# Seven more seven-product couples in the down products of a two-layer encoder trunk, all weights' sums prepared ahead, and the preparation's transfers on GpSimd's queue

## The chip, the cores and the metric

The kernel runs on one core of a Trainium2 chip. The metric is the device time of one execution in microseconds (us). Three runs of the kernel before took 2364.60, 2366.93 and 2368.82 us; the median is 2366.93 us. One further execution was profiled.

## The reference

The model is a trunk of two layers on one sequence of 256 tokens with 2048 channels, all in float32. Each layer has a token mixer (layer 0 a bidirectional mLSTM, layer 1 a bidirectional gated linear recurrence) and then a convolutional gated MLP, each behind an RMSNorm and added to the residual:

```python
def conv_glu(hn, w_up, conv_w, conv_b, w_down):
    u = hn @ w_up                       # 2048 -> 2 x 5504
    a, v = jnp.split(u, 2, axis=-1)
    ...                                 # c: centred depthwise convolution of width 3 over a
    return (jax.nn.gelu(c, approximate=False) * v) @ w_down      # 5504 -> 2048

for layer in range(DEPTH):
    ...
    h = h + mix
    h = h + conv_glu(rmsnorm(h, norm_ffn_g[layer]), ...)
return rmsnorm(h, final_g)
```

The change touches the last product, `@ w_down`, which is called the down product below; its input (256 tokens by 5504) is called g.

## The kernel before, in words

**Three matmuls for one product.** Every operand x is split into a high part xh (fp32r) and a low part xl = x - xh. A product of x and w is the sum of xh·wh, xh·wl and xl·wh, three matmuls of 128 x 512 on TensorE (L236). Activations are split when they are made. Weights are split as they arrive: a raw piece of 128 x 1024 floats is copied to wh by ScalarE (L147) and wl = raw - wh is taken by VectorE (L148). A helper keeps pieces ahead of TensorE, in four buffers for wh and wl each and, in the MLP, two more.

**Chunks and stages.** TensorE's work is a list of chunks. In an MLP the 43 blocks of 128 hidden channels come in two parts of 22 and 21. Each part first has one up chunk for each block, and then two down chunks, each for 1024 of the 2048 output columns; two such down chunks that follow each other are a pair of chunks, and there are four pairs of chunks in all (two layers, two parts).

**Couples and seven products.** A down chunk (`squares_by_seven`) takes two blocks of g at a time, a couple. The 256 tokens x 256 channels of a couple and its 256 x 1024 weights form 2 x 2 squares, A11 to A22 and B11 to B22. A plain couple takes eight products, 24 matmuls, into the four accumulators C11, C12, C21, C22. A couple that is listed in `SEVEN` takes seven products, 21 matmuls, by a Strassen-Winograd scheme: P1, P6, P7 and P5 go to four accumulators of their own, and three go straight to C11, C12 and C21. It needs sums of the activations' squares S1 to S4 (`token_sums`) and sums of the weights' squares T2, T3, T4 and B12 - B11. The accumulators are PSUM banks: P1, P6, P7, P5 in four banks of the pool `psm` (tiles named mm), C11 to C22 in four of `psa` (tiles named pc). The eight banks are all there are, so the next chunk's accumulators can begin only when the last ones have been read out.

**Reading out.** When a down chunk has met its last seven-product couple, `mid` (L584 to L592) adds the four P banks into the residual hm: ScalarE copies P1 to u (L584), VectorE adds P1, P6, P5 (twice), u and P7 in six instructions of 128 x 512 (L585 to L590), GpSimd adds u to two squares of hm (L591, L592). At the end of the chunk `done` adds C11, C21, C12 and C22 on VectorE (L598). In the kernel before, `mid` is called with one plain couple (nine or ten couples in, of eleven) still to come.

**Where the weights' sums come from.** Either on the fly: four VectorE subtractions (L207) right before the couple, listed in `FLY`; or prepared: earlier, while an up stage or the mixer runs, the couple's raw weights (two transfers of 512 KB into tiles praw) are loaded, four subtractions are made on VectorE (L632), and the result is stored to a scratch tensor tscr (two transfers of 512 KB, L635). When the couple comes, three transfers bring 768 KB of raw weights, 768 KB of sums (tile T, L198) and 256 KB more (L199).

**Order.** Instructions are written in program order with a planner's ticks for the side work (`Side`); a list scheduler that works on an estimated timeline then sets the order on each engine. Each engine runs its instructions in that order. All weights' loads and, before the change, all transfers of the preparation inside the MLP are issued by SyncE (SP), which also issues in order and waits in order. There, loads of the preparation are pinned among the loads of up weights (`late`, L395).

## Time and profile before

| what | value |
|---|---|
| three runs, us | 2364.60, 2366.93, 2368.82 |
| profiled execution, span from first to last instruction | 2364.5 us |
| granted TensorE clock, mean | 0.999 |
| up stages (layer 0 part 0 and 1, layer 1 part 0 and 1), from us | 388.7, 742.1, 1663.7, 2017.3 |
| pairs of down chunks, from us | 634.2, 975.1, 1909.3, 2250.3 |
| DMA, mean over the span | 268 GB/s, 632.97 MB |
| instructions | 38407 |

The profile gives one time for the profiled execution, its span; no time around it is listed. A row of a group view has the line, the engine, the operation, the tiles (written <- read) and their shapes, the count, then busy us and the mean ns of one, then the idle time before it and what ended it. A row of the view by windows gives, for each engine, busy us and the number of instructions that ran, then the granted clock, the busy share of the 16 DMA engines, and GB/s. A row of the timeline has start in us, duration in us, engine, line, operation, tiles, count.

### The profile page before, as it was taken

The numbers are of one execution on the slowest core, as the hardware profiler recorded it, in microseconds if no ns is written. First come the engines' busy times: TensorE is split into PE (matmuls) and PEld (weight loads), VectorE is DVE, ScalarE is ACT, GpSimd is POOL, SyncE is SP. The second block draws the span as 40 slices with busy tenths as digits, with TensorE's granted clock in tenths as the row PEclk, the third lists the DMA queues.
The fourth block names the chain that finished last, engine by engine and source line by source line (L and its number), as shares of the span: only waits on it lengthen the run. The fifth ranks groups of instructions, "written<-read, shape, count | busy, mean of one in ns | idle before, by whom it ended". The sixth has DMA issues, their size and how long they took to land. (4 is left out here: it accounts for less than half of the span.)

```text
span 2364.5 us, 38407 instructions
## 1 busy us (share of the span) xinstructions
PE 2354.1 (100%) x14545; PEld 2016.2 (85%) x14545; DVE 1993.5 (84%) x3087; ACT 1470.0 (62%) x2340; POOL 196.5 (8%) x244
## 2 busy tenths in 40 slices
PE   9999999999999999999999999999999999999998
PEld 8888888888888888888888888888888888888887
DVE  7777687888998898897888888778789889888888
ACT  7655456555665555676777777776555567455565
POOL 0100000000000000000232322220000000000000
PEclk9999999999999999999999999999999999999999
DMA  8776656888888878996556665646788888888896
GB/s 303 239 248 242 213 195 211 295 282 292 313 321 327 306 282 292 330 334 230 208 203 223 212 225 204 214 169 228 270 300 289 289 321 335 295 287 302 309 351 221
DMA packets 122266, 632.97 MB, mean 268 GB/s; under 512 B 13776, under 2 KB 14928, under 8 KB 77664
## 3 DMA queue, kind: packets, MB, share of 16 engines
q1 hardware_dynamic: 120384, 626.51, 75.0%
q0 software_dynamic: 1120, 3.21, 0.8%
q8 instruction: 114, 1.87, 0.3%
q10 hardware_dynamic: 576, 0.79, 0.1%
q14 instruction: 72, 0.59, 0.1%
HBM read 562.24 MB, written 68.22 MB: 267 GB/s over the span
## 5 line engine op out<-in xcount | busy, mean ns | idle before, releaser
L357 PE MATMUL mm<-xt,wh 128*128 128x512 f32 x3776 | 1312.0, 394 | 0.0
L148 DVE TENSOR_TENSOR wl<-raw,wh 128x1024 fp32r<-128x1024 f32 (+1 forms) x844 | 1037.3, 1234 | 222.6 <-ACT wh L147 214.5
L147 ACT CAST wh<-raw 128x1024 fp32r<-128x1024 f32 (+1 forms) x844 | 875.3, 1042 | 513.0 <-PE mm L357 305.8
L361 PE MATMUL mm<-xt,wl 128*128 128x256 f32 x3776 | 1043.5, 278 | 0.0
L357 PEld LDWEIGHTS mm<-xt,wh 128*128 128x128 f32 x3776 | 705.6, 188 | 160.6 <-issue 0.4
L361 PEld LDWEIGHTS mm<-xt,wl 128*128 128x128 f32 x3776 | 709.4, 188 | 4.5
L373 PE MATMUL mm<-wh,xt 128*128 128x512 f32 x1024 | 324.4, 392 | 0.6 <-ACT wh L147 0.5
L236 PE MATMUL pc<-wh,g 128*128 128x512 f32 (+1 forms) x716 | 243.2, 388 | 0.3 <-ACT wh L147 0.2
L373 PEld LDWEIGHTS mm<-wh,xt 128*128 128x128 f32 x1024 | 191.2, 188 | 40.0 <-ACT wh L147 1.1
L632 DVE TENSOR_TENSOR praw<-praw 128x512 f32<-128x512 f32 x252 | 174.1, 691 | 44.7 <-DMA praw<-in_w_d 29.0
L373 PE MATMUL mm<-wl,xt 128*128 128x512 f32 x512 | 199.7, 391 | 0.0
L236 PEld LDWEIGHTS pc<-wh,g 128*128 128x128 f32 x716 | 134.1, 188 | 29.0 <-ACT wh L147 1.5
L236 PE MATMUL mm<-wh,sx 128*128 128x512 f32 x432 | 153.4, 389 | 0.0
L148 DVE TENSOR_TENSOR wl<-T,wh 128x1024 fp32r<-128x1024 f32 (+1 forms) x144 | 135.9, 955 | 13.3 <-ACT wh L147 8.9
L147 ACT CAST wh<-T 128x1024 fp32r<-128x1024 f32 (+1 forms) x144 | 118.6, 835 | 44.7 <-DMA T<-tscr 18.2
L236 PE MATMUL pc<-wl,g 128*128 128x512 f32 (+1 forms) x358 | 138.8, 388 | 0.0
L591 POOL TENSOR_TENSOR hm<-hm,u 128x512 f32<-128x512 f32 x10 | 14.8, 1481 | 1223.8 <-DVE u L590 1223.8
L373 PEld LDWEIGHTS mm<-wl,xt 128*128 128x128 f32 x512 | 96.2, 188 | 18.6
L1071 DVE TENSOR_TENSOR QK<-QK,G 128x256 f32<-128x256 f32 x224 | 104.6, 515 | 6.2 <-ACT kq L1050 5.9
L1195 ACT COPY avc<-mm 128x256 f32<-128x256 f32 x172 | 64.0, 372 | 63.9 <-PE mm L361 63.6
L1050 ACT COPY kq<-QK 128x512 f32<-128x512 f32 x112 | 74.5, 669 | 37.3 <-DVE QK L1071 29.5
L236 PEld LDWEIGHTS mm<-wh,sx 128*128 128x128 f32 x432 | 81.0, 188 | 16.9 <-ACT wh L147 0.2
(246 smaller groups left out, 2263.1 us busy)
## 6 DMA issues: line engine op xcount, KB each, us to landing
raw<-in_w_up SPq DMA_DIRECT2D x172, 1024.0 KB, 6.1
tscr<-praw SPq DMA_DIRECT2D x126, 512.0 KB, 6.7
praw<-in_w_d SPq DMA_DIRECT2D x120, 512.0 KB, 6.8
raw<-in_w_bq SPq DMA_DIRECT2D x48, 1024.0 KB, 5.0
T<-tscr SPq DMA_DIRECT2D x63, 768.0 KB, 7.6
raw<-in_w_d SPq DMA_DIRECT2D x60, 768.0 KB, 6.0
raw<-in_w_ao SPq DMA_DIRECT2D x24, 1024.0 KB, 4.8
raw<-in_w_d SPq DMA_DIRECT2D x24, 1024.0 KB, 7.7
```

The source lines that it names most:

```text
L147: pin(act.copy(wh[:, :m], r))
L148: pin(dve.tensor_tensor(wl[:, :m], r, wh[:, :m].bitcast(F32), ALU.subtract))
L236: pin(pe.matmul(ps, a, b, start=bank not in begun, stop=stop and i == 2))
L357: hold(pe.matmul(ps[f], wh[:, c:c + P], x, start=k + kk == 0, stop=False))
L361: hold(pe.matmul(ps[f][:, 0:T], wl[:, c:c + P], x[:, 0:T], start=False, stop=k + kk == ch.nk - 1))
L373: pe.matmul(ps[t], x[:, a + t * P:a + (t + 1) * P], w[:, c], start=st and i == 0, stop=sp and i == 2)
L591: pool.tensor_tensor(part(1, 0), part(1, 0), u, ALU.add)
L632: dve.tensor_tensor(out, x, y, ALU.subtract)
L1050: act.copy(m, blocks(QK, h))
L1071: dve.tensor_tensor(two[:, j], two[:, j], by[:, j], ALU.mult)
L1195: act.copy(z, p[:, T:2 * T])
```

## The change

Five things change together.

- `SEVEN` now lists, for each of the four pairs of chunks, the couples of its first and of its second down chunk apart. Before, both chunks of a pair had the same list; there were 2 x (9 + 8 + 9 + 7) = 66 couples. Now there are 10 + 10, 9 + 8, 10 + 10 and 9 + 7, which is 73. In part 0 of either layer the last couple of the chunk, number 10 of 0 to 10, is now a seven-product couple. In part 1 the chunk ends with a single block, and the couple before it is now one.
- `FLY` is gone: no sums on the fly. Six couples of the down chunks were made so; all 73 are now prepared.
- In a last seven-product couple the order of products is P1, P6, P7, P5, then `mid`, then the three that go to C (in part 1 C12 stands behind P1). The first couple of a chunk takes its four accumulators in the order C22, C12, C11, C21. C22 can stop at the last plain couple.
- The preparation in the MLP issues its transfers on GpSimd's queue (`pool.dma_start`, 122 loads and 122 stores), and loads two items ahead, each after the store that frees its buffer.
- To make room, `ones` shrinks to 128 columns, R has one buffer, gs shares the tile jk; where only one chunk of a pair uses a couple's sums, they get a tile of their own ("spare").

```diff
-SEVEN = ((1, 2, 3, 4, 5, 6, 7, 8, 9), (1, 2, 3, 4, 5, 6, 7, 8)), ((1, 2, 3, 4, 5, 6, 7, 8, 9), (1, 2, 3, 4, 5, 6, 7))
-FLY = (2,), (5,), (2,), ()
+SEVEN = (range(1, 11), range(1, 11)), (range(1, 10), range(1, 9)), (range(1, 11), range(1, 11)), (range(1, 10), range(1, 8))
 FIRST = 6
-SPLIT = (0, 2, 5), (0, 2, 5)
+SPLIT = 2, 1
...
         units, last = (ch.nk + 1) // 2, max(ch.seven)
+        alone = max(set(range(units)) - set(ch.seven))
...
-                    product(ps, x, w, u == last and ps in psm_)
+                    product(ps, x, w, u == last if ps in psm_ else end)
                     side.tick(0.65)
...
             if u in ch.seven:
                 S1, S3, S2, S4 = ch.sums(u)
-                products((P1, A11, B11), (C12, S4, B22))
+                products((P1, A11, B11))
+                if not end:
+                    products((C12, S4, B22))
                 T2, T3 = piece()
                 products((P6, S2, T2), (P7, S3, T3))
                 B21, T1 = piece()
-                products((C11, A12, B21), (P5, S1, T1))
-                T4, _ = piece()
-                products((C21, A22, T4))
+                products((P5, S1, T1))
                 if u == last:
                     ch.mid(psm_)
                     ch.rest = ch.ends
+                if end:
+                    products((C12, S4, B22))
+                products((C11, A12, B21))
+                T4, _ = piece()
+                products((C21, A22, T4))
                 continue
             B21, B12 = piece()
-            for ps, (x, w), (y, v) in ((C11, (A11, B11), (A12, B21)), (C12, (A11, B12), (A12, B22)),
-                                       (C21, (A21, B11), (A22, B21)), (C22, (A21, B12), (A22, B22))):
+            both = [(C11, (A11, B11), (A12, B21)), (C12, (A11, B12), (A12, B22)),
+                    (C21, (A21, B11), (A22, B21)), (C22, (A21, B12), (A22, B22))]
+            for ps, (x, w), (y, v) in [both[i] for i in ((3, 1, 0, 2) if u == 0 else range(4))]:
                 product(ps, x, w, False)
-                product(ps, y, v, end)
+                product(ps, y, v, end or ps is C22 and u == alone)
...
+        put = start if ahead else nc.sync.dma_start
         yield first
         load(0)
+        if ahead:
+            load(1)
         for i, (_, dst) in enumerate(todo):
             yield period / 2
-            if ahead:
-                load(i + 1)
...
             for j in range(2):
-                nc.sync.dma_start(dst[:, j * 1024:(j + 1) * 1024], loaded[i][j])
+                put(dst[:, j * 1024:(j + 1) * 1024], loaded[i][j])
+            if ahead:
+                load(i + 2)
             yield period / 3
...
-                                  todo, 18.0, (nf * 10.4 - 26.0) / len(todo), finished, late, True))
+                                  todo, 18.0, (nf * 10.4 - 26.0) / len(todo), finished, pool.dma_start, True))
```

**Place 1: VectorE at the end of the first down chunk of layer 0, part 0.** Tiles mm_6313 to mm_6316 are P1, P6, P7, P5 of the ending chunk and pc_6317 to pc_6320 its C11, C12, C21, C22; hm is the residual; wl_6726 and wl_6743 are the next chunk's first two weight pieces. Before:

```order
L585 TENSOR_TENSOR hm_75<-hm_75,mm_6313 128x512
L586 TENSOR_TENSOR u_6732<-u_6732,mm_6314 128x512
L587 TENSOR_TENSOR hm_75<-hm_75,mm_6316 128x512
L589 TENSOR_TENSOR hm_75<-hm_75,mm_6316 128x512
L588 TENSOR_TENSOR hm_75<-hm_75,u_6732 128x512
L148 TENSOR_TENSOR wl_6726<-raw_6723,wh_6725 128x1024
L590 TENSOR_TENSOR u_6732<-u_6732,mm_6315 128x512
L598 TENSOR_TENSOR hm_75<-hm_75,pc_6317 128x512
```

Now, where mm_6362 to mm_6365 are P1, P6, P7, P5, pc_6366 to pc_6369 are C11, C12, C21, C22, and wl_6790 and wl_6800 are the next chunk's first two pieces, wl_6828 and wl_6847 those behind them:

```order
L591 TENSOR_TENSOR hm_75<-hm_75,mm_6362 128x512
L593 TENSOR_TENSOR hm_75<-hm_75,mm_6365 128x512
L595 TENSOR_TENSOR hm_75<-hm_75,mm_6365 128x512
L147 TENSOR_TENSOR wl_6790<-raw_6787,wh_6789 128x1024
L604 TENSOR_TENSOR hm_75<-hm_75,pc_6366 128x512
L592 TENSOR_TENSOR u_6806<-u_6806,mm_6363 128x512
L147 TENSOR_TENSOR wl_6800<-raw_6787,wh_6799 128x1024
L594 TENSOR_TENSOR hm_75<-hm_75,u_6806 128x512
L147 TENSOR_TENSOR wl_6828<-raw_6822,wh_6827 128x1024
L147 TENSOR_TENSOR wl_6847<-T_6824,wh_6846 128x1024
L596 TENSOR_TENSOR u_6806<-u_6806,mm_6364 128x512
L604 TENSOR_TENSOR hm_75<-hm_75,pc_6367 128x512
```

The adds of P5 (mm_6365) come second and third, and everything behind them waits for P5's last matmul; the next chunk's second piece, wl_6800, stands behind four adds, and the adds of P6 and C are mixed with the new pieces.

**Place 2: TensorE at the same end.** Before, P5 (mm_6316) stops here, 26 matmuls of the last, plain couple follow, and then the next chunk begins with pc_6787; the last of these rows are

```order
L236 MATMUL pc_6320<-wl_6714,g20_6191 128x512
L236 MATMUL pc_6320<-wh_6713,g20_6191 128x512
L236 MATMUL pc_6320<-wh_6703,g21_6310 128x512
L236 MATMUL pc_6320<-wl_6704,g21_6310 128x512
L236 MATMUL pc_6320<-wh_6703,g21_6310 128x512
L236 MATMUL pc_6787<-wh_6725,g0_4006 128x512
```

Now the first row is P5's last matmul, nine matmuls follow, and the next chunk begins with pc_6845, whose bank is that of pc_6366:

```order
L235 MATMUL mm_6365<-wh_6773,sx_6353 128x512
L235 MATMUL pc_6366<-wl_6774,g21_6350 128x512
L235 MATMUL pc_6366<-wh_6773,g21_6350 128x512
L235 MATMUL pc_6368<-wh_6780,g21_6350 128x512
L235 MATMUL mm_6363<-wl_6764,sx_6353 128x512
L235 MATMUL mm_6363<-wh_6763,sx_6353 128x512
L235 MATMUL mm_6364<-wl_6764,sx_6353 128x512
L235 MATMUL mm_6364<-wh_6763,sx_6353 128x512
L235 MATMUL pc_6368<-wl_6781,g21_6350 128x512
L235 MATMUL pc_6368<-wh_6780,g21_6350 128x512
L235 MATMUL pc_6845<-wh_6799,g0_4006 128x512
L235 MATMUL mm_6838<-wh_6827,g2_4224 128x512
```

Between P5's last matmul and the next chunk's first there are 9 matmuls where there were 26.

**Place 3: VectorE at the end of the first down chunk of layer 0, part 1**, which closes with a single block of twelve matmuls. mm_9646 to mm_9649 are P1, P6, P7, P5; pc_9650 is C11; wl_10047 and wl_10067 are the next chunk's first two pieces. Now:

```order
L592 TENSOR_TENSOR u_10053<-u_10053,mm_9647 128x512
L593 TENSOR_TENSOR hm_75<-hm_75,mm_9649 128x512
L595 TENSOR_TENSOR hm_75<-hm_75,mm_9649 128x512
L594 TENSOR_TENSOR hm_75<-hm_75,u_10053 128x512
L147 TENSOR_TENSOR wl_10047<-raw_10044,wh_10046 128x1024
L147 TENSOR_TENSOR wl_10067<-raw_10044,wh_10066 128x1024
L596 TENSOR_TENSOR u_10053<-u_10053,mm_9648 128x512
L604 TENSOR_TENSOR hm_75<-hm_75,pc_9650 128x512
```

On TensorE 17 matmuls stand between P5's last matmul there and the first one that writes to the bank of pc_9650. Before, there was a plain couple between the last seven-product couple and the single block, and 38 matmuls stood between P5's last one and the next chunk's first one that reads its first block of g.

34 lines of the change are left out of this document (20 added, 14 removed).

## The prediction

> **What bounds the kernel now.** I read the page first, then TensorE's waits, then the windows of the stages, then the timeline at the places that the change rewrites.
>
> ```profile
> span 2364.5 us, 38407 instructions
> PE 2354.1 (100%) x14545; PEld 2016.2 (85%) x14545; DVE 1993.5 (84%) x3087; ACT 1470.0 (62%) x2340; POOL 196.5 (8%) x244
> PE idle L1266 <- POOL ones L1259: 1.1, 1, 1.1
> PE mm L236 <- DVE wl L148: 0.5, 1, 0.5
> PE mm L373 <- ACT wh L147: 0.5, 2, 0.3
> PE pc L236 <- ACT wh L147: 0.2, 1, 0.2
> ```
>
> TensorE is busy all the time. Its waits add up to 2.3 us in 2364.5, and only 0.7 of them are in the down product (L236). So the time is TensorE's list of matmuls: one matmul less is a gain of its whole step, and a wait that the change makes is paid in full, for there is no slack on TensorE in which it could vanish. What else is full shows in the windows (the pairs of down chunks of layer 0 part 0 and of layer 1 part 0, the first up stage, and 20 us in each of the two pairs):
>
> ```profile
> 634.20:742.10 107.90, 107.83 (x476) 88.95 (x475) 99.29 (x112) 73.18 (x86) 3.54 (x2) 1.00 0.86 321
> 1909.30:2017.30 108.00, 107.78 (x476) 88.80 (x475) 102.50 (x117) 72.93 (x87) 3.55 (x2) 1.00 0.88 325
> 388.70:634.20 245.50, 245.50 (x1421) 214.76 (x1420) 213.81 (x349) 141.12 (x223) 0.70 (x1) 1.00 0.85 294
> 650.00:670.00 20.00, 20.00 (x90) 16.57 (x89) 16.64 (x17) 14.56 (x18) 0.00 (x0) 1.00 1.01 405
> ```
>
> In a pair of down chunks VectorE is busy 99.29 of 107.90 us and 102.50 of 108.00, the DMA engines 0.86 and 0.88. Neither stops TensorE on average, but neither has much left for a crowded moment. The step of a 128x512 matmul is 107.9 / 476 = 0.2267 us (a record is longer, 0.39, since matmuls overlap). The clock is 1.00 throughout, so it makes no difference here.
>
> **The change part by part.** *Matmuls removed.* Seven couples go from 24 to 21 matmuls: 21 x 0.2267 = **-4.8 us**, all of it on TensorE. That is the whole prize.
>
> *On-the-fly sums removed.* TensorE loses time at two of the six couples that were made on the fly:
>
> ```profile
> 699.59 0.61 PE L236 MATMUL mm<-wh,sx 128*128 128x512 f32 x2
> 700.28 0.50 PE L236 MATMUL pc<-wh,g 128*128 128x512 f32 x1
> 700.62 0.40 PE L236 MATMUL mm<-wh,sx 128*128 128x512 f32 x1
> 1930.43 0.69 PE L236 MATMUL mm<-wh,sx 128*128 128x512 f32 x2
> 1931.33 0.50 PE L236 MATMUL pc<-wh,g 128*128 128x512 f32 x1 [0.22 <-ACT wh L147]
> 1931.67 0.40 PE L236 MATMUL mm<-wh,sx 128*128 128x512 f32 x1
> ```
>
> Three steps take 1.03 and 1.24 us there instead of 0.68: 0.35 + 0.56 lost, **-0.9 us**. A stall also costs about 0.11 after it (the step behind it is 0.34, not 0.227). The other four couples lose nothing now, so nothing comes back there.
>
> *Preparation of 13 more couples, in the up stages.* Four units or three more per stage, each with four subtractions on VectorE:
>
> ```profile
> L632 DVE TENSOR_TENSOR praw<-praw 128x512 f32<-128x512 f32 x252 | 174.1, 691 | 44.7 <-DMA praw<-in_w_d 29.0
> ```
>
> At 0.691 us, 16 more are 11 us; the added token sums make some 2 to 3 more. VectorE goes from 213.8 to about 227 of 245.5 us: it fits, TensorE covers it, cost **0**. Without that cover a stage would pay up to the 13 us.
>
> *Transfers moved to GpSimd.* 244 issues of 512 KB leave SP's queue. GpSimd issues the same kind of instruction now, in the mixer (group row, then the timeline of GpSimd and VectorE at one of them):
>
> ```profile
> L820 POOL DMA_DIRECT2D Mb<-mscr x16 | 8.7, 549 | 65.2 <-DVE W L824 59.2 <-DVE rd L852 3.3 <-DMA mscr<-M 2.7
> 142.09 1.11 POOL L820 DMA_DIRECT2D Mb<-mscr  x2 [45.43 <-DVE W L824]
> 141.70 1.22 DVE L148 TENSOR_TENSOR wl<-raw,wh 128x1024 fp32r<-128x1024 f32 x1
> ```
>
> An issue holds GpSimd for 0.55 us, 61 of them 33 us in an up stage where it works for 0.70. The wl instruction that runs beside two of them is 1.22 us, as everywhere. Lower bound 0; upper bound, if VectorE stood still for each issue, is a rival below. I take **0**: the row beside it decides. SP loses waits of its queue and can only be earlier with weights.
>
> [...]
>
> *The end of a down chunk.* This is where I expect the cost. Before, a plain couple stood between P5 and the next chunk. VectorE needed from 681.98 to 689.3 for the reading out (TensorE's P5 ends with the row of 681.91):
>
> ```profile
> 681.91 0.39 PE L236 MATMUL mm<-wh,sx 128*128 128x512 f32 x1
> 681.98 0.68 DVE L586 TENSOR_TENSOR u<-u,mm 128x512 f32<-128x512 f32 x1
> 682.58 0.68 DVE L587 TENSOR_TENSOR hm<-hm,mm 128x512 f32<-128x512 f32 x1
> 683.17 0.68 DVE L589 TENSOR_TENSOR hm<-hm,mm 128x512 f32<-128x512 f32 x1
> 683.77 0.69 DVE L588 TENSOR_TENSOR hm<-hm,u 128x512 f32<-128x512 f32 x1
> 684.37 1.22 DVE L148 TENSOR_TENSOR wl<-raw,wh 128x1024 fp32r<-128x1024 f32 x1
> 685.51 0.68 DVE L590 TENSOR_TENSOR u<-u,mm 128x512 f32<-128x512 f32 x1
> 686.11 0.68 DVE L598 TENSOR_TENSOR hm<-hm,pc 128x512 f32<-128x512 f32 x1
> 686.70 2.04 DVE L148 TENSOR_TENSOR wl<-raw,wh 128x1024 fp32r<-128x1024 f32 x1
> 688.66 0.68 DVE L598 TENSOR_TENSOR hm<-hm,pc 128x512 f32<-128x512 f32 x1
> 689.26 1.72 DVE L148 TENSOR_TENSOR wl<-T,wh 128x1024 fp32r<-128x1024 f32 x1
> ```
>
> An add starts 0.60 us after the one before it and is 0.68 long; a weight piece holds VectorE for 1.14 and is 1.22 long. C11's bank (first L598) was free at 686.79; the next chunk was due 27 steps behind P5, at 681.91 + 6.1 = 688.0. No wait, 1.2 us to spare.
>
> Now I put the same durations on the new order (place 1 of the change). Let 0 be the start of P5's last matmul. With that record's 0.39 and some 0.05 to signal, VectorE's first add of P5 starts at 0.44, the second at 1.04, wl_6790 at 1.64, C11's add (pc_6366) at 2.78, and it ends at 3.46. TensorE comes to the new chunk's first matmul, which takes that bank, after 10 steps, at 2.27, and can start at 3.5: **wait 1.2**. VectorE goes on: L592 at 3.38, wl_6800 from 3.98 to 5.20; TensorE needs that piece two steps behind its start, at 3.95: **wait 1.3**. Then L594 at 5.12, wl_6828 from 5.72 to 6.94, needed seven matmuls later (6.79): 0.15; wl_6847 ends at 8.08, needed two more steps on (7.41): 0.7; pc_6367's bank is free at 9.29, needed five on (9.2): 0.1. Together **3.4 us**: 7.3 us of VectorE's work that had 6.1 us of TensorE's cover now have 2.3, and the next pieces queue behind them.
>
> At the same place of part 1 (place 3): adds at 0.44, 1.04, 1.64, pieces at 2.25 and 3.39, L596 at 4.53, C11's add from 5.13 to 5.82. TensorE arrives after 18 steps, at 4.09: **wait 1.8**. Layer 1's order is nearly the same; I take the same figures. Where a pair ends and an up stage follows, the next chunk's first matmuls use other data and I find no wait in the order. So 2 x (3.4 + 1.8) = **+10.4 us**, and some 12 single waits at 0.11 each behind them, **+1.3**.
>
> *GpSimd beside VectorE in that crowd.* In the rows above two pieces took 2.04 and 1.72 us instead of 1.22, while GpSimd added u:
>
> ```profile
> 686.36 1.30 POOL L591 TENSOR_TENSOR hm<-hm,u 128x512 f32<-128x512 f32 x1 [293.55 <-DVE u L590]
> 687.62 2.28 POOL L592 TENSOR_TENSOR hm<-hm,u 128x512 f32<-128x512 f32 x1
> ```
>
> That is 1.3 us more on VectorE for each `mid`. Before, it lay beside TensorE's cover; now part of it falls into the chain. Between 0 and 4 x 1.3 I take **+1.0**, since L596, which releases GpSimd, is last in the chain, when most of the waits are past.
>
> [...]
>
> *Sum.* 2364.5 - 4.8 - 0.9 + 10.4 + 1.3 + 1.0 = 2371.5 us of span. The median of the runs shown is 2366.9, 2.4 above the profiled span, so I predict **2373.9 us**, 0.3% slower. About 0.2%, 4.7 us, is what a measurement of this kernel can tell from no change.
>
> **Rivals.**
>
> *Only the banks wait.* My chain takes VectorE's order as rigid, with each instruction as late as its predecessor makes it. If TensorE's first wait of 1.2 lets VectorE catch up so that the weight pieces are in time, only the waits for C11's bank stay: 2 x (1.2 + 1.8) = 6.0 and 0.7 behind them. SP's queue, without the preparation's stores, may also remove a stall of 0.8 at the start of the last pair (two steps in 1.27):
>
> ```profile
> 2260.86 0.40 PE L236 MATMUL pc<-wh,g 128*128 128x512 f32 x1
> 2261.79 0.50 PE L236 MATMUL mm<-wl,g 128*128 128x512 f32 x1 [0.53 <-DVE wl L148]
> 2262.13 0.40 PE L236 MATMUL mm<-wh,g 128*128 128x512 f32 x1
> ```
>
> 2364.5 - 4.8 - 0.9 - 0.8 + 6.7 = 2364.7, at the runs' level 2367: no difference that can be measured. Against it: VectorE is busy 92% and the pieces behind the bank stand in its order one by one.
>
> *The ends are hidden.* If the adds of P1, P6 and P7 are done early and the C adds pass, only the gains stay: 2364.5 - 4.8 - 0.9 = 2358.8, or **2361.2**, faster by 0.24%. For it: six P and C adds cost 3.6 us of VectorE in sum, and the new order stops C22 early. Against it: P5 itself is only 9 matmuls (2.0 us) from the end, and its two adds come ahead of the C add in the order.
>
> *DMA becomes the bound in part 0.* A seven-product couple moves more bytes than a plain one (1 MB):
>
> ```profile
> T<-tscr SPq DMA_DIRECT2D x63, 768.0 KB, 7.6
> raw<-in_w_d SPq DMA_DIRECT2D x60, 768.0 KB, 6.0
> raw<-tscr SPq DMA_DIRECT2D x63, 256.0 KB, 6.5
> ```
>
> 1792 KB, 1.835 MB. A chunk of ten such couples and a plain one moves 19.4 MB where it moved 17.8, a pair 38.8 MB, and its 468 matmuls take 106.1 us: 366 GB/s. Today's pair ran at 325 GB/s with a share of 0.88, so a full share is worth about 369, and the window above reached 405 for 20 us. If 5% of the 369 are lost (351 GB/s), a pair needs 110.5 us, 4.4 more, in two pairs 8.8: 2373.9 + 8.8 = **2383**. The point from which it decides is 366 GB/s. In the 20 us at 650 the DMA share was full and TensorE didn't wait, which speaks against it; buffers ahead of TensorE carried that stretch, and a whole pair is longer.
>
> *GpSimd's issues stop VectorE.* Then 33 us come onto VectorE's 227 in each up stage, 260 of 245.5: +15, four times +58, some **2430**. The wl row of 1.22 us speaks against it.
>
> **How the numbers follow.** The forecast, with waits for banks and for pieces at the first chunks' ends, 0.43, between 2369 and 2380 by its own (without the waits for pieces of 0.15 and less, and without the 1.0; with the full 1.3 at each of the four ends and layer 1 a little worse). Only banks 0.27; hidden 0.18; DMA 0.09; GpSimd 0.03. Of "only banks", part falls under 2362.2, and of "hidden" part above it, about alike. The forecast and the last two are slower by over 0.2%, less a bit of the forecast under 2371.7: slower 0.53, same 0.28, faster 0.19. The range goes from 2359, which leaves out the lower part of "hidden", to 2385, which holds most of the DMA case.
>
> **What would show it.** Right: in TensorE's waits, at the first chunk's end of each pair, L235 behind VectorE (the C add, L604, and the piece, L147), 3 to 4 us in part 0 and about 2 in part 1; TensorE's matmuls take 4.8 us less; no wait inside the couples that were on the fly. Wrong: no such wait (hidden); waits for pieces anywhere in the middle of a part-0 pair, behind a DMA (DMA); an up stage longer than before with VectorE's rows stretched (GpSimd). The largest single risk is the 2 x 3.4: it stands on an order and on durations of other instructions, not on a trace of that place.

## The result

The changed kernel takes **2383.84 us** (median of four runs, 2380.67 to 2388.43) where the kernel before takes 2367.66 (four runs). The ratio is 1.0068, 95% interval 1.0055 to 1.0080: slower by 16 us. The prediction was 2373.9, slower, with a range of 2359 to 2385. So the side was right and the time is inside the range, but the loss of 7 us was less than half of the measured one.

The profiled execution is the slowest of the four (2388.43 us, span 2386.7). A later execution of the same kernel was traced too (e11, 2378.11 us, span 2376.3), and the two differ by 10 us. Both are needed below: what is the same in both is set by the order of the instructions, the rest is not.

The span and the waits of TensorE in the changed kernel's trace (us in total, times, longest):

```profile
span 2386.7 us, 38736 instructions
PE 2361.1 (99%) x14524; PEld 2015.2 (84%) x14524; DVE 2020.6 (85%) x3159; ACT 1486.4 (62%) x2364; POOL 324.4 (14%) x488
PE pc L235 <- DVE hm L604: 4.3, 3, 1.6
PE mm L367 <- DVE wl L147: 2.8, 2, 2.1
PE mm L235 <- ACT wh L146: 2.1, 3, 1.3
PE mm L235 <- DVE wl L147: 1.7, 4, 0.8
PE mm L235 <- DVE u L596: 1.0, 1, 1.0
PE pc L235 <- DVE wl L147: 0.9, 1, 0.9
PE mm L235 <- DVE hm L595: 0.9, 1, 0.9
```

TensorE waited 0.7 us in the down product before; now the rows of L235 alone make 10.9. There are three kinds: the C banks (L604) and P banks (L595, L596) that VectorE has not read out, pieces of weights behind VectorE and ScalarE, and, new and not in the down product at all, L367, a wait of 2.1 us in an up stage.

The next table is worked out from TensorE's timeline: in each stage, the sum over its matmuls of the time from start to start, less the plain step (0.227 us in the down stages, 0.231 + 0.115 for a pair in the up stages). It includes the pauses, the longer steps behind them and everything slow. "d" is a pair of down chunks, "u" an up stage, 1 to 4 in the order of the program (d1 and d3 are part 0).

| lost, us | u1 | d1 | u2 | d2 | u3 | d3 | u4 | d4 |
|---|---|---|---|---|---|---|---|---|
| before | 1.0 | 0.3 | 0.4 | 0.1 | 1.0 | 0.5 | 0.4 | 1.0 |
| the change | 0.9 | 4.6 | 6.4 | 2.2 | 0.9 | 6.7 | 5.2 | 2.2 |
| the change again (e11) | 0.9 | 4.6 | 0.4 | 2.1 | 0.9 | 8.4 | 0.6 | 2.5 |

For the first trace: 29.1 - 4.7 = 24.4 us lost more, 4.8 saved by 21 matmuls, and the rest, 2.6 us, lies outside these stages, 1.4 of it between d2 and u3, where the mixer of layer 1 runs; together 22.2, the difference of the spans (2386.7 - 2364.5). For e11 it is 20.4 - 4.7 = 15.7, less 4.8, with 0.9 outside these stages: 11.8, the difference of the spans.

**The ends of the first down chunks.** TensorE and then VectorE of the changed kernel at the end of the first chunk of d1, the place that the prediction worked out:

```profile
687.40 0.39 PE L235 MATMUL pc<-wh,g 128*128 128x512 f32 x1
688.95 0.47 PE L235 MATMUL pc<-wh,g 128*128 128x512 f32 x1 [1.16 <-DVE hm L604]
689.26 0.40 PE L235 MATMUL mm<-wh,g 128*128 128x512 f32 x1
690.60 0.50 PE L235 MATMUL pc<-wl,g 128*128 128x512 f32 x1 [0.94 <-DVE wl L147]
693.47 0.50 PE L235 MATMUL mm<-wl,sx 128*128 128x512 f32 x1 [0.40 <-DVE wl L147]
698.22 0.50 PE L235 MATMUL mm<-wl,sx 128*128 128x512 f32 x1 [0.76 <-DVE wl L147]
```

```profile
688.13 0.68 DVE L604 TENSOR_TENSOR hm<-hm,pc 128x512 f32<-128x512 f32 x1
689.32 1.22 DVE L147 TENSOR_TENSOR wl<-raw,wh 128x1024 fp32r<-128x1024 f32 x1
692.20 1.22 DVE L147 TENSOR_TENSOR wl<-T,wh 128x1024 fp32r<-128x1024 f32 x1
695.86 2.30 DVE L147 TENSOR_TENSOR wl<-raw,wh 128x1024 fp32r<-128x1024 f32 x1
```

The row at 687.40 is the old chunk's last matmul and 688.95 the new one's first: 1.55 us from start to start, 1.32 more than a step, while VectorE's add of C11 ends at 688.81. The next, 1.11, is the chunk's second piece (VectorE's row of 689.32). Then 0.57 at 693.47, and 0.93 at 698.22, for a piece that took 2.30 us instead of 1.22.

**The up stage u2.** TensorE, VectorE and GpSimd's queue at the long wait there:

```profile
870.21 0.40 PE L363 MATMUL mm<-xt,wh 128*128 128x512 f32 x1
872.66 0.39 PE L367 MATMUL mm<-xt,wl 128*128 128x256 f32 x1 [2.06 <-DVE wl L147]
874.03 0.63 PE L363 MATMUL mm<-xt,wh 128*128 128x512 f32 x1
```

```profile
865.22 0.42 DVE L1216 TENSOR_TENSOR g<-avc,g 128x256 fp32r<-128x256 f32 x1
869.78 0.69 DVE L639 TENSOR_TENSOR praw<-praw 128x512 f32<-128x512 f32 x1 [4.15 <-issue]
```

```profile
861.98 0.53 POOL L627 DMA_DIRECT2D praw<-in_w_d  x1 [3.64 <-DMA tscr<-praw]
871.85 0.53 POOL L627 DMA_DIRECT2D praw<-in_w_d  x1 [9.34 <-DMA tscr<-praw]
```

GpSimd issued a load of the preparation at 861.98, after 3.64 us in which it waited for a store to free the buffer. VectorE stands for 4.15 us in front of the subtraction L639 that needs such a load, with the next weight piece behind it in its order; TensorE runs out of pieces and waits 2.06 us. The name of the releaser ("issue") doesn't tell it; that it is the load follows from the operands.

### The profile page after: what moved, and what is told of

It is laid out like the page before. It is cut to its first block, busy times and chain, and to the rows that moved or that the text cites. A ratio compares the mean times of both kernels' runs of the same rounds, so it can differ in the third digit from the quotient of the medians.

```text
span 2386.7 us, 38736 instructions
## 1 busy us (share of the span) xinstructions
PE 2361.1 (99%) x14524; PEld 2015.2 (84%) x14524; DVE 2020.6 (85%) x3159; ACT 1486.4 (62%) x2364; POOL 324.4 (14%) x488
## 4 chain that ended last, share of the span: by engine, by line
PE 93%; DVE 2%; DMA 2%; issue 2%; ACT 0%; POOL 0%; SPq 0%; DVEq 0%; POOLq 0%; ACTq 0%
PE mm L363 36%; PE mm L379 18%; PE mm L367 18%; PE pc L235 10%; PE mm L235 8%; DVE wl L147 1%; DMA praw<-in_w_d 1%; PE pn L858 1%; PE py L1117 1%; PE pd L1067 0%; PE pz L440 0%; ACT wh L146 0%; PE pa L1067 0%; DMA T<-tscr 0%; DMA raw<-in_w_d 0%
## 5 line engine op out<-in xcount | busy, mean ns | idle before, releaser
L367 PE MATMUL mm<-xt,wl 128*128 128x256 f32 x3776 | 1047.5, 279 | 3.3 <-DVE wl L147 2.8
L367 PEld LDWEIGHTS mm<-xt,wl 128*128 128x128 f32 x3776 | 711.0, 188 | 8.2 <-DVE wl L147 3.6
L639 DVE TENSOR_TENSOR praw<-praw 128x512 f32<-128x512 f32 x304 | 209.9, 693 | 44.4 <-issue 23.1
L235 PE MATMUL pc<-wh,g 128*128 128x512 f32 (+1 forms) x640 | 225.5, 389 | 4.3 <-DVE hm L604 4.3
L235 PE MATMUL mm<-wh,sx 128*128 128x512 f32 x474 | 167.1, 390 | 3.4 <-ACT wh L146 1.5
L147 DVE TENSOR_TENSOR wl<-T,wh 128x512 fp32r<-128x512 f32 (+1 forms) x158 | 148.7, 960 | 18.7 <-ACT wh L146 18.3
L146 ACT CAST wh<-T 128x512 fp32r<-128x512 f32 (+1 forms) x158 | 129.4, 835 | 48.4 <-PE mm L235 15.2
L235 PEld LDWEIGHTS pc<-wh,g 128*128 128x128 f32 x640 | 119.6, 188 | 31.0 <-ACT wh L146 3.7
L627 POOL DMA_DIRECT2D praw<-in_w_d x122 | 65.5, 537 | 562.4 <-DMA tscr<-praw 365.9
L235 PE MATMUL pc<-wl,g 128*128 128x512 f32 (+1 forms) x320 | 124.3, 388 | 0.9 <-DVE wl L147 0.9
L642 POOL DMA_DIRECT2D tscr<-praw x122 | 65.6, 538 | 322.7 <-DVE praw L639 237.0
L235 PEld LDWEIGHTS mm<-wh,sx 128*128 128x128 f32 x474 | 88.8, 188 | 23.3 <-ACT wh L146 2.6
```

Of the source, the lines that this page charges most:

```text
L146: pin(act.copy(wh[:, :m], r))
L147: pin(dve.tensor_tensor(wl[:, :m], r, wh[:, :m].bitcast(F32), ALU.subtract))
L235: pin(pe.matmul(ps, a, b, start=bank not in begun, stop=stop and i == 2))
L367: hold(pe.matmul(ps[f][:, 0:T], wl[:, c:c + P], x[:, 0:T], start=False, stop=k + kk == ch.nk - 1))
L627: start(r[j], todo[i][0][:, j * 1024:(j + 1) * 1024])
L639: dve.tensor_tensor(out, x, y, ALU.subtract)
```

## The experiments

Each comparison was made against the kernel before on the same chip; its medians there lie between 2367.16 and 2368.20 us, so a difference between two experiments is good to about 1 us beside their own spread. Losses by stage of all of them, made as in the table above:

| lost, us | u1 | d1 | u2 | d2 | u3 | d3 | u4 | d4 |
|---|---|---|---|---|---|---|---|---|
| e1 preparation on SyncE | 1.0 | 8.1 | 0.4 | 2.6 | 3.2 | 8.8 | 1.3 | 4.0 |
| e2 only the queue | 1.2 | 0.9 | 0.4 | 0.1 | 0.9 | -0.1 | 5.2 | -0.1 |
| e3 couples undone | 1.3 | -0.1 | 0.4 | 0.1 | 1.4 | -0.1 | 2.9 | 0.4 |
| e4 shifted couples | 1.0 | 4.2 | 0.4 | 6.9 | 1.6 | 9.0 | 0.4 | 2.6 |
| e5 no P adds at the ends | 0.9 | 6.1 | 1.5 | 0.1 | 0.9 | 1.4 | 4.4 | 1.6 |
| e6 12 prepared a stage | 0.9 | 4.6 | 0.4 | 2.1 | 0.9 | 7.5 | 2.0 | 2.0 |
| e7 loads SyncE, stores GpSimd | 4.6 | 10.4 | 0.4 | 3.0 | 8.0 | 9.4 | 0.4 | 5.4 |
| e9 e5 and e6 together | 2.6 | 4.6 | 4.9 | 0.1 | 0.9 | 1.5 | 0.8 | 1.4 |
| e10 e3, all 73 prepared | 0.9 | -0.1 | 0.4 | 0.1 | 0.9 | -0.1 | 1.2 | 0.4 |
| e12 e5 without one couple's sums | 0.9 | -0.1 | 5.5 | 0.1 | 0.9 | -0.1 | 0.8 | 0.9 |

### Which part of the change costs: e1 to e3

The first theory after the two traces (A) had two causes: VectorE's crowd at the ends, and GpSimd's queue in the up stages of part 1.

e1 undoes the queue alone:

```diff
-        put = start if ahead else nc.sync.dma_start
         load(0)
-        if ahead:
-            load(1)
...
             yield period / 2
+            if ahead:
+                load(i + 1)
...
-                put(dst[:, j * 1024:(j + 1) * 1024], loaded[i][j])
-            if ahead:
-                load(i + 2)
+                nc.sync.dma_start(dst[:, j * 1024:(j + 1) * 1024], loaded[i][j])
...
-                                  todo, 18.0, (nf * 10.4 - 26.0) / len(todo), finished, pool.dma_start, True))
+                                  todo, 18.0, (nf * 10.4 - 26.0) / len(todo), finished, late, True))
```

> The changed kernel with one part undone: the preparation's transfers are issued by SyncE again, one item ahead, as in the kernel before; the 73 couples and their order stay. Theory A (late preparation on GpSimd's queue costs the up stages of part 1 their 5.9 and 4.8 us, the ends of the first down chunks cost about 12.7): the up stages are back at 233 us, the waits at the ends stay, about 2373 us. Theory B (13 more prepared couples are too much for the up stages, whoever issues their transfers): still a wait behind VectorE and a long up stage in part 1, 2380 to 2385 us.

Measured: 2393.99 us, ratio 1.0102 (1.0089 to 1.0116), **slower still than the change**, and above what either theory said. The up stages of part 1 are indeed back (u2 0.4, u4 1.3), and the waits at the ends are there (1.10, 0.28, 0.37, 0.93 and 1.40 us in d1). But pauses appear early in the part-0 pairs (1.0, 1.9 and 0.4 us between 646 and 655) and at the end of u3. A view of SyncE's waits shows what came back to its queue:

```profile
SPq L641 <- DVE praw L638: 150.6, 73, 6.3
```

73 times, 150.6 us in all, SyncE stands before a store until VectorE has subtracted, and weights' transfers queue behind it. The kernel before has the same row, though, and lost nothing by it:

```profile
SPq L635 <- DVE praw L632: 123.3, 91, 5.9
```

So moving the preparation to GpSimd was worth about 10 us to the 73 couples; that these waits are the reason is argued, not shown. (The profiled execution took 2387.3 us, the other three 2394; what those had more was not traced.)

e2 does the queue alone, on the kernel before (the diff above the other way round).

> The kernel before with only the move of the preparation's transfers to GpSimd, two items ahead; couples, sums on the fly and order of products as before. Theory A: the late preparation comes with the queue, so up stages of part 1 get longer by 4 to 6 us each: 2372 to 2379 us. Theory B (the number of couples): with 12 items in a stage nothing is late, 2365 to 2369 us, no difference.

Measured: 2367.89 us, ratio 0.9999 (0.9990 to 1.0008): no difference. Theory A, with its 2372 to 2379, missed. In the trace u4 does lose 5.2 us behind a pause of 1.37 us (VectorE stood 4.70 us before a subtraction whose load came late), but d3 and d4 gain 1.7.

e3 undoes the couples and leaves all else:

```diff
-SEVEN = (range(1, 11), range(1, 11)), (range(1, 10), range(1, 9)), (range(1, 11), range(1, 11)), (range(1, 10), range(1, 8))
+SEVEN = (range(1, 10), range(1, 10)), (range(1, 9), range(1, 9)), (range(1, 10), range(1, 10)), (range(1, 9), range(1, 8))
```

> The changed kernel with the seven new couples taken back (1 to 9 twice, 1 to 8 twice, in layer 1 1 to 8 and 1 to 7: 66 couples), all of them prepared, on GpSimd's queue. Theory A: the waits at the ends of the first down chunks go (12.7 us), 21 matmuls come back (4.8 us), the losses of the up stages stay: about 2376 us, and no wait of 1 us or more behind VectorE within 20 us of a change of down chunks. If the ends cost nothing, 2384 + 4.8 = 2389 us.

Measured: 2367.62 us, ratio 0.9998 (0.9990 to 1.0007); theory A's 2376 missed. The edit leaves 67 couples, not 66: it takes back six of the seven, and the first chunk of d4 keeps one more than before (1 to 8, where it had 1 to 7), with a plain couple behind it. No wait is left at the ends, and the up stages lose far less than expected. So the **whole loss hangs on the six couples at the ends of chunks**: without them, new queue, new order of products and no sums on the fly are worth nothing that was measured and cost nothing.

### The ends: e5 and e4

e5 leaves out `mid` in the first chunk of each pair:

```diff
         def mid(ps):
+            if c0 == 0 and nk > KT:
+                return
             P1, P6, P7, P5 = ps
```

> The changed kernel; the first down chunk of each pair leaves out the nine adds of the P banks into the residual (mid), so its output is another one. Theory A (the ends wait for VectorE's crowd of P adds, C adds and weight pieces): the waits behind VectorE at the four ends, 11 to 13 us in the changed kernel's trace, shrink to 0 to 3 us; about 2374 us. Theory C (the pieces at the ends are late because their transfers are late): the waits stay, 2382 to 2386 us.

Measured: 2376.11 us, ratio 1.0040 (1.0026 to 1.0054), 7.7 us less than the change. Some of TensorE's waits of this kernel, whose lines behind the edit are two higher (the P adds are L593 to L598, the C add L606):

```profile
PE mm L235 <- ACT wh L146: 4.0, 3, 3.2
PE mm L367 <- DVE wl L147: 1.4, 2, 0.7
PE pc L235 <- DVE wl L147: 0.5, 1, 0.5
PE mm L235 <- DVE wl L147: 0.2, 1, 0.2
PE pz L440 <- DVE hm L606: 0.3, 1, 0.3
```

No wait of the down product for a C or P add is left (the one of 0.3 us is of a transpose in a norm), and d2 falls from 2.2 to 0.1. Theory A holds for the ends: it is VectorE's queue, not late weights. In d1 the gain is hidden, since a wait of 3.2 us behind ScalarE came up at another place, 16 us into the pair; more on that below.

e4 keeps 73 couples but shifts them, so that the plain couple is the last one, with the preparation on SyncE as in e1:

```diff
-SEVEN = (range(1, 11), range(1, 11)), (range(1, 10), range(1, 9)), (range(1, 11), range(1, 11)), (range(1, 10), range(1, 8))
+SEVEN = (range(0, 10), range(0, 10)), (range(0, 9), range(0, 8)), (range(0, 10), range(0, 10)), (range(0, 9), range(0, 7))
```

> 73 couples as in the change, but shifted by one so that the plain couple is the last one (0 to 9 twice, 0 to 8 and 0 to 7, in layer 1 0 to 9 twice, 0 to 8 and 0 to 6), preparation issued by SyncE as before. Theory A: 36 matmuls stand between P5's last one and the next chunk again, and the next chunk begins with a bank of P1 that has long been read; no waits at the ends, no late preparation, 21 matmuls less: 2361 us. If the new couples cost time in another way than by the ends (bytes from memory, VectorE's share), 2368 to 2375 us.

Measured: 2386.29 us, ratio 1.0080 (1.0066 to 1.0093), above both ranges. The ends are nearly cured (one pause of 1.1 us in d1, one of 1.2 in d3, none in d2), and the loss has moved to the starts: pauses of 1.2, 5.0 and 3.8 us as d1, d2 and d3 begin. SyncE and ScalarE of this kernel there:

```profile
981.46 5.58 SPq L197 DMA_DIRECT2D T<-tscr  x3
```

```profile
987.82 1.04 ACT L146 CAST wh<-T 128x1024 fp32r<-128x1024 f32 x1 [1.58 <-DMA T<-tscr]
```

The sums of the pair's second couple are loaded to a tile T that is one of three temporaries of the up stage, and the last blocks of the up stage still hold them. When the first couple is plain, it bridges that time. This reading comes from the kernel's text and these rows; no run takes the tile away here. By the time measured, the first couple of a pair is as bad a place for a seven-product couple as the last one.

### The up stages: e6, e7, e10

e6 keeps all 73 couples in the down chunks, but prepares only 12 in a stage:

```diff
     def store(ch, src, u, todo):
+        if len(todo) >= 12:
+            ch.stored[u] = todo[len(todo) - 12 + turns["a"] % 12][1]
+            turns["a"] += 1
+            return
         ch.stored[u] = tscr[turns["t"]]
```

> The changed kernel with its 73 couples and its order, but only 12 couples are prepared in each up stage; the couples beyond that take another couple's stored sums, so its output is another one. Bytes and instructions of the down chunks stay. Theory A (15 preparations in a part-1 up stage are too many for the loop of store, load and subtraction on GpSimd's queue): up stages of part 1 are 233 to 235 us instead of 238.9 and 237.7, the ends wait as before, about 2374 us. Theory D (GpSimd's queue is late with any number): still 237 us or more in the up stages, 2380 to 2386 us.

Measured: 2380.51 us, ratio 1.0058 (1.0044 to 1.0071). The up stages lose 0.4 and 2.0 instead of 6.4 and 5.2, as theory A wants, but the time is only 3 us less, a third of what it said; and e11, which prepares everything, lost 0.4 and 0.6. The ends in d1 are the same within 0.003 us (1.32, 1.11, 0.57, 0.93).

e10 is e3 with the preparation of all 73 couples, six of them unused (it has 67 couples too):

```diff
+USED = (range(1, 10), range(1, 10)), (range(1, 9), range(1, 9)), (range(1, 10), range(1, 10)), (range(1, 9), range(1, 8))
...
-                ch = pair(src, nf, c0, lambda k: GT[k], lambda u: SX[u], norm, seven)
+                used = USED[2 * layer + part][c0 // 2]
+                ch = pair(src, nf, c0, lambda k: GT[k], lambda u: SX[u], norm, used)
...
+                for u in set(ch.stored) - set(used):
+                    ch.stored.pop(u)
```

> The 66 couples of e3 with the preparation of all 73: the seven more couples are loaded, subtracted and stored in the up stages, and not used. Theory A (the number of preparations makes them late): up stages of part 1 at 236 to 239 us, no waits at the ends, 2371 to 2378 us. If the preparation alone is harmless and only the longer couple lists hurt: 2365 to 2369 us as e3.

Measured: 2366.56 us, ratio 1.0001 (0.9992 to 1.0010). Here this half of **theory A falls**: the number of preparations is harmless by itself.

e7 splits the queues: loads from SyncE, stores from GpSimd.

```diff
-                nc.sync.dma_start(dst[:, j * 1024:(j + 1) * 1024], loaded[i][j])
+                (pool if ahead else nc.sync).dma_start(dst[:, j * 1024:(j + 1) * 1024], loaded[i][j])
```

(This one is shown against e1.)

> The changed kernel, with the preparation's loads issued by SyncE as before the change (pinned, one item ahead) and only its stores by GpSimd, so that no load stands behind a store in GpSimd's queue and no store that waits for VectorE stands in SyncE's. Theory A (what is late is late in a queue): up stages of part 1 at 233 us, no waits at the starts of the down pairs, ends as before, about 2373 us. Theory E (the bytes are too many, however issued): one of the two losses stays, 2380 us or more.

Measured: 2401.83 us, ratio 1.0143 (1.0128 to 1.0158), the slowest of all. u2 and u4 are clean at 0.4, but u1, u3 and every pair are worse, with pauses of 2.6 us in d1, 3.5 at the end of u3 and 2.4 in d3. Theory A's number is missed. Theory E's is met (2380 or more, and the loss in the pairs stays), but not for its reason: e12 below moves the same bytes through the down pairs without a loss there. In d1 and d3 ScalarE waited 3.87 and 4.58 us for a late load of a tile T (the same waits in e1 are 3.25 and 4.21 us), and at the end of u3 4.50 us for the pair's first raw weights. Why these loads go out late is open here: that a load on SyncE stands before a store's release, now on another queue, is only argued.

### What e5 had left: e9, e11, e12

e9 joins e5 and e6.

> The changed kernel with both suspects taken away: the first down chunk of each pair leaves out its nine P adds, and only 12 couples are prepared in each up stage (the others take another couple's sums), so its output is another one. If the waits at the ends and the late preparation are the whole loss, what stays is 21 matmuls and the stalls of the on-the-fly couples less: 2361 to 2364 us, faster than before. If the bytes of the ten-couple chunks cost time in themselves, waits behind transfers stay in the down pairs of part 0, 2368 to 2374 us.

Measured: 2377.77 us, ratio 1.0045 (1.0032 to 1.0058), no better than e5 alone, and above both ranges. So there is a third cause. In d1 and d3 TensorE paused 2.8 and 0.9 us, 16 and 17 us into the pair.

e11, the change again:

> The changed kernel once more, for a second trace. What is set by the order must come again: the waits at the ends of the first down chunks within 0.1 us of the first trace (1.32, 1.11, 0.57 and 0.93 at the first one). What is set by transfers may move: the up stages of part 1 between 233 and 239 us.

The execution took 2378.11 us. At the end of d1 the first two waits came again (1.324 and 1.109 us both times), as did those of d2 (1.752 and 1.754 in sum) and d4 (1.658 and 1.664). The third and fourth of d1, 0.57 and 0.93, did not: there TensorE ran eight steps that were 0.20 us longer each (see the last section), and d1 lost 4.6 us all the same. That fits VectorE's queue setting the time at this place: a slower TensorE came no later. The up stages of part 1 were at 233.0 and 233.1. In d3 a pause of 1.53 us came at 1931.2, where the first trace has 1.47 at 1938.7. That is 18 us behind the pair's start in both, and so it is set by the order too. ScalarE and SyncE of the first trace, d3 starting at 1921.2:

```profile
1939.30 1.57 ACT L146 CAST wh<-T 128x1024 fp32r<-128x1024 f32 x2 [4.54 <-DMA T<-tscr]
```

```profile
1908.09 0.33 SPq L197 DMA_DIRECT2D T<-tscr  x1
1920.92 0.32 SPq L197 DMA_DIRECT2D T<-tscr  x1
1932.05 0.86 SPq L197 DMA_DIRECT2D T<-tscr  x2
1936.23 0.43 SPq L197 DMA_DIRECT2D T<-tscr  x1
```

The third load of T goes out 10.8 us into the pair, and ScalarE waits 4.54 us for it. In e10's trace (d3 from 1909.4) the third goes out 3.3 us into the pair, and nothing waits. What holds the tile is visible in e5, whose d1 starts at 634.1 (ScalarE):

```profile
645.72 0.52 ACT L574 CAST sx<-avc 128x384 fp32r<-128x384 f32 x1 [0.44 <-DVE avc L573]
647.65 0.30 ACT L577 CAST g<-avc 128x128 fp32r<-128x128 f32 x1 [1.42 <-DVE avc L573]
652.69 1.04 ACT L146 CAST wh<-T 128x1024 fp32r<-128x1024 f32 x1 [4.73 <-DMA T<-tscr]
```

Couple 10 of part 0 is made of the last two blocks, and it is new among the seven-product couples. Its token sums (sx, from avc) are still being made 12 to 14 us into the down pair, in one of the three temporaries that T needs.

e12 takes that away from e5:

```diff
-                    SX[i // 2] = token_sums(mp, n, box["c"], c, avc[:, 0:2 * T], z)
+                    SX[i // 2] = SX[9] if i // 2 == 10 else token_sums(mp, n, box["c"], c, avc[:, 0:2 * T], z)
```

> The kernel of e5 (no P adds at the first chunks' ends), with one thing more: couple 10 of part 0 makes no token sums of its own but takes those of couple 9, so its output is another one, and the last block's temporary tile, from which tile T of the next couples is cut, is free earlier. Theory F (the token sums of couple 10 hold that tile, so that the third load of T in a part-0 pair is issued 10 to 11 us into the pair instead of 3 to 6, and TensorE waits for it some 18 us in): that load comes within 7 us of the pair's start, the waits at 650 and 1934 us of e5 (3.4 and 0.75 us, 5.6 and 1.2 with what follows) are gone, 2369 to 2371 us. If those waits come from the mere bytes of the couples' weights, they stay: 2375 to 2378 us.

Measured: 2370.39 us (11 runs), ratio 1.0010 (1.0001 to 1.0019), as theory F said. That is 2.2 us over the kernel before on the same chip, where e5 was 8.6 over: 6.4 us less. SyncE around the start of d3 (at 1913.7):

```profile
1900.62 0.33 SPq L197 DMA_DIRECT2D T<-tscr  x1
1913.45 0.32 SPq L197 DMA_DIRECT2D T<-tscr  x1
1917.07 0.42 SPq L197 DMA_DIRECT2D T<-tscr  x1
1924.60 0.84 SPq L197 DMA_DIRECT2D T<-tscr  x2
```

The third load is back at 3.4 us, and d1, d2 and d3 lose nothing at all. The bytes of the ten-couple chunks, the same in e5 and e12, need no time of their own. What e12's trace still loses is mostly u2, 5.5 us, with two short waits and a slow rhythm all through; without those 5 us its span (2366.4) would be 2361.4, 2.6 above the 2358.8 that 21 matmuls less and no sums on the fly should give. Of these, 2.1 lie between d2 and u3, and their cause is open.

### A pause alone: e8

The rhythm of TensorE was an open question, since u2 and u4 lost more than their pauses.

```diff
+                if layer == 0 and f == 8:
+                    for _ in range(2):
+                        pin(dve.tensor_tensor(hm[:, :, :], hm[:, :, :], hm[:, :, :], ALU.max))
                 GT.append(g)
```

> The kernel before, with two long VectorE instructions of 128 x 4096 (the residual's maximum with itself, which changes nothing) behind the ninth block of the first up stage, so that TensorE waits there once for a weight piece. If a pause alone sets TensorE's slower rhythm (pairs of matmuls at 353.3 ns instead of 346.7, as behind the pauses of the changed kernel), the pairs behind this pause take 353 ns to the end of the stage, 134 us later, and cost 2 to 3 us beside the wait itself. If the rhythm comes from GpSimd's transfers, the pairs are back at 346.7 ns within 10 us.

A single execution: 2369.02 us. VectorE's two instructions are 4.42 us each, at 501.58 and 509.45, and the wait that was meant did not come: no step of TensorE there is more than 0.01 us over the plain one. Yet from 515.6 to the end of the stage, 121 us later, the pairs take 353 ns, and u1 loses 3.3 us where it lost 1.0. Two windows of this kernel, before and behind that point:

```profile
480.00:500.00 20.00, 20.00 (x118) 17.47 (x117) 17.64 (x30) 11.56 (x19) 0.00 (x0) 1.00 0.82 283
540.00:560.00 20.00, 20.00 (x115) 17.31 (x115) 18.08 (x34) 11.61 (x20) 0.00 (x0) 1.00 0.80 278
```

TensorE is busy in both, at clock 1.00, but does 118 matmuls in the one and 115 in the other. GpSimd does nothing in either. So the slow rhythm needs neither GpSimd's transfers nor a pause. What it does need this run doesn't tell.

## Why the prediction was right or wrong

**What bounds the kernel:** right. TensorE's list is the time, every wait is paid; the saved matmuls are saved (each stage with more couples has its 3 matmuls less for each).

**The end of a down chunk:** right, nearly term by term. In d1 the forecast had 1.2 for C11's bank, 1.3 for the second piece, 0.7 for a later one; the trace has 1.32, 1.11 and 0.57, and e5 shows that it is VectorE's queue. The two smallest (0.15, 0.1) are within the unevenness of the steps. For a signal the forecast took 0.05; the first add of P5 began 0.04 us behind the end of P5's last record (685.75 to 685.79), the matmul of the second piece 0.06 behind the piece (690.54 to 690.60), and the one that takes C11's bank 0.14 behind the add (688.81 to 688.95). In part 1 the forecast 1.8 is 1.75 in d2 and 1.66 in d4. d3 was taken like d1; in detail it is another list (0.78, 1.03, 0.37, 0.47, 0.27, 1.28 us), with the sum 4.2. With the longer steps behind the waits the ends of the first trace make 13.2 us (4.6 + 2.2 + 4.7 + 1.7), against 10.4 + 1.3 + 1.0 = 12.7. That the sums are so near is in part luck: by the three terms it is 9.3 for the waits, 1.7 for the steps behind them and 2.2 for GpSimd.

**GpSimd beside VectorE in that crowd:** right in kind. The row of 695.86, 2.30 us instead of 1.22, is behind L596, and the wait of 0.93 follows from it; in d3 the same place has 1.28. 1.0 was taken, and these two make 2.2. GpSimd's rows at the first place:

```profile
694.10 1.29 POOL L597 TENSOR_TENSOR hm<-hm,u 128x512 f32<-128x512 f32 x1 [121.33 <-DVE u L596]
695.35 1.73 POOL L598 TENSOR_TENSOR hm<-hm,u 128x512 f32<-128x512 f32 x1
```

They run from 694.10 to 697.08; VectorE's piece of 695.86 (2.30 us) begins beside them. The next piece of 128 x 1024, at 698.68, is behind their end and took 1.21. What the runs show is the longer row; what makes it longer was not shown.

**On-the-fly sums and matmuls:** the sum -5.7. Both stalls of before are gone; in the trace of e3, which has this gain (-0.9), one of the seven new couples and the new queue, d1 and d3 lose 0.4 and 0.6 us less than before, while its time shows no difference: 0.9 is below what a comparison could tell. The second stall (1931.33), though, was misread. The sums on the fly of that chunk were made by 1917.7, 14 us earlier; what came late there was a prepared couple. ScalarE of the kernel before:

```profile
1929.28 1.05 ACT L147 CAST wh<-T 128x1024 fp32r<-128x1024 f32 x1 [3.36 <-DMA T<-tscr]
```

ScalarE waited 3.36 us for a load of a tile T. This is the kind of wait that the prediction then left out, and it stood in the trace before the change.

**What failed** are two terms that were put at nothing, "preparation of 13 more couples" (it fits, cost 0) and "transfers moved to GpSimd" (0); and for the first 20 us of a part-0 pair the forecast has no term at all. That the time still lies in the range is luck: the forecast by itself went from 2369 to 2380, and the range reached 2385 for a full DMA, which did not come. Two things were not seen:

- *The token sums of the new couple.* They were costed as 2 to 3 us of VectorE somewhere in the up stage. But couple 10 of part 0 comes from the last two blocks, so its sums run into the down pair, and they hold one of three temporaries that the tile T of the next couples needs. The price is a pause of 1.5 us in d3 in both traces of the change, up to 3.4 in d1 in others; e12 against e5 puts it at 6.4 us where both pairs have it. The DMA rival had such waits in the middle of a part-0 pair behind a transfer, but for another reason: it is a late issue, not a full DMA, and e12 with the same bytes has none of it.
- *The preparation in GpSimd's queue can come late.* The issues don't slow VectorE's instructions, as was argued from the wl row of 1.22: that row is 1.22 us on the mean in u1 before and after the change. But a load of a buffer waits in GpSimd's queue for the store before it (3.64 us at 861.98), and VectorE then stands before the subtraction (4.15 us at 869.78) with weight pieces behind it. In the first trace that cost 2.2 and 1.0 us of pauses, and u2 and u4 lost 10.7 us more than before with what followed them; in e11 nothing. It happens with the queue and 66 couples too (u4 of e2), and it is not set by the number of preparations (e10).

Of the 22 us between the first trace and the one of before, the ends and the saved matmuls were foreseen (13.2 - 4.8). Of the rest, 1.9 is the late T, 10.7 is what u2 and u4 lost more, and 2.6 us lie outside these stages, with a cause that is open; against these, some 1.4 us of what the pairs lost before is gone. Of the 16.2 us between the medians the split can't be told so exactly: each against the kernel before on its own chip, e5 says 7.6 for the ends (less than the 13 of the traces, since e5's own d1 got a long T wait in exchange), e12 6.4 for the sums of couple 10 on top of it, and with both taken away 2.2 us are still lost where 5.7 should be gained. These 8 us stay open in part; what e12's u2 loses, 5 us, and the 2.1 us between d2 and u3 are the pieces that a trace shows.

**The clock** was said to make no difference. It does behind some pauses (see the last section): 1.7 us of the 6.4 in u2 of the first trace, and 1.6 of the 8.4 in d3 of e11. At the end of d1 of e11 the slow steps only took the place of two waits.

## What to carry to other kernels

The place of an operation in a chain of stages can be worth more than its count: 21 matmuls less gave 4.8 us, and took 13 at the end of a chunk, where the reading out of banks lost its cover, and more at the start of it, where the new couple's inputs held a buffer that the next transfers needed. For an edit at a boundary, write down both neighbours: what the last instructions read out and who waits for those banks, and which buffers the last producers hold and who needs them next. Where the order was at hand row by row, with durations from the trace (d1 and d2), the first waits of such a chain were worked out to 0.2 us; a buffer's holder and a queue that waits in order have to be looked up in the same way, and not to be taken as free because an engine's share leaves room.

## What the runs showed of the hardware

**Two rhythms of TensorE.** In the up stages a pair of matmuls (512 and 256 columns wide) takes 346.7 ns on the mean, or 353.2 to 353.4, over stretches of up to 230 us; the granted clock is 1.00 in both. The kernel before had only the fast one in its up stages, apart from their first 15 us. The slow one begins at different moments: when TensorE was held up, be it 2.06 us (u2 of the change) or 0.1 (u4, at 2078.8), or as the stage begins (u2 of e12), or behind VectorE's long instructions with no step more than 0.01 us over the plain one (e8), and stays to the end of the stage or to another such moment (in e3 it was fast again behind a pause at 2107). Not each pause starts it (u4 of e6 and of e10 stayed fast). It costs 1.9%, here up to 4.5 us in a stage. What makes it is open: the order of steps is then a cycle of three pairs (232, 118, 240, 120, 236, 114 ns).

**The clock behind a pause.** Three windows of the change, before the wait of 2.06 us, behind it, and later; the number before the DMA share is the granted clock:

```profile
868.00:870.00 2.00, 2.00 (x13) 1.76 (x12) 0.22 (x1) 1.05 (x1) 0.00 (x0) 1.00 0.99 416
872.60:876.40 3.80, 3.74 (x13) 3.16 (x14) 3.80 (x10) 2.38 (x6) 1.08 (x2) 0.56 0.89 295
877.00:880.00 3.00, 3.00 (x19) 2.58 (x18) 3.00 (x7) 1.73 (x5) 0.00 (x0) 1.00 0.92 317
```

And one of e11, behind the second wait at the end of d1:

```profile
690.90:694.50 3.60, 3.60 (x11) 2.82 (x10) 3.60 (x5) 0.00 (x0) 0.73 (x1) 0.53 0.87 288
```

Behind the wait of 2.06 us TensorE ran at 0.56 for 3.8 us: a matmul of 512 columns took 426 ns from start to start instead of 231. That added 1.7 us to a pause of 2.2. The pauses of 1.75 us in d2 and 1.66 in d4 had no such aftermath (the granted clock of both pairs is 1.00); those of 1.3 and 1.1 right behind each other in d1 had none in the first trace (690.9 to 694.5, clock 1.00) and had it in e11 (the same stretch, clock 0.53). In d1 of e5, behind a pause of 3.4 us, 12 matmuls from 653.79 to 659.16 took 5.37 us, the last nine of these steps 426 ns each. So it came behind a single wait of 2.06 us, and behind the same pair of waits once and once not; what decides was not shown.
